# Seven block products in place of eight for gate and up of the last 1024 tokens of an encoder layer

## The chip, the cores and the metric

The kernel runs on one core of one Trainium2 chip, as one program of 36,635 instructions. The metric is the device time of one execution in microseconds (us); before the change the median of three runs is 2945.6 us (2943.91 to 2950.24).

## The reference, cut to what matters

One encoder layer over 2048 tokens with 1024 channels, all in float32: three mixers (a top-k latent attention, a gated linear attention and a sliding-window attention), an output projection, and then a feed-forward block with 2816 inner channels. The change touches the feed-forward block alone:

```python
x = x + jnp.concatenate([out_a, out_b, out_c], axis=-1) @ w_out
h = rms_norm(x, norm_ffn)
x = x + (jax.nn.silu(h @ w_ffn_gate) * (h @ w_ffn_up)) @ w_ffn_down
return rms_norm(x, final_norm)          # D_MODEL 1024, D_FF 2816, SEQ 2048
```

## The kernel before, in words

**Tiles.** Channels lie on the 128 partitions and tokens along the free axis. A group is 512 tokens; there are four groups. Every large product is done to nearly float32 precision by three matmuls: each operand is split into a part `hi`, rounded to the type that TensorE takes (float32r), and the rest `lo`, and hi·hi, lo·hi and hi·lo are summed in PSUM (L175 to L177 for the products over 8 blocks of input channels, L299 to L301 for the down projection). The split of a tile of 128x512 is one cast on ScalarE (L116) and one subtraction on GpSimd (L119). `square`, `norm_scale` and `finish` are the pieces of the RMS norm.

**Stages.** First come the projections and the mixers of all groups (`pass1`, `pass2`). The top-k attention (`dsa`: `select` and `attend` of 16 blocks of 128 queries) runs beside them and beside the feed-forward blocks of groups 0 and 1, which are done one group at a time, with tiles named `mf` in PSUM. The function `merge` interleaves these two threads by their estimated costs. When all 16 blocks are attended, the memory of the first part is given back, and the feed-forward block of groups 2 and 3 runs alone, with both groups in one pass (`halves` of 512 tokens, `W` = 1024, tiles named `pf`). This is the last stage.

**Inside `ffn`.** First `w_out` is applied and the residual added (L215 to L218), for half 0 and then for half 1; `normed` (L220) scales and splits the result into the operands `h2` of a half: a multiplication on VectorE (L229), a cast on ScalarE (L231), a subtraction on GpSimd or VectorE (L232), eight times. Then 22 steps `gate_up(f)`, each for 128 inner channels: 24 matmuls for gate and 24 for up, per half; tanh on ScalarE (L277), two combinations on VectorE (L278, L283) and the split of the result into `fh` and `fl`. `down` (L287) takes two steps at a time and adds to the residual `x2` on VectorE (L302).

**Weights.** The first feed-forward block (group 0) loads each weight tile, 128x512 float32, splits it and stores the halves, 512 KB, in DRAM; all later blocks load the stored halves (L131), into 5 buffers beside the attention and 9 in the last stage. All DMAs go through SyncE's queue. A weight tile of gate or up serves 12 matmuls per half.

**Order.** The program issues its instructions in the order of the generators, but each engine's queue is arranged when the kernel is built, by what is ready, with the program's order as priority; the queues are then run strictly in that arranged order.

## Time and profile before

| | us |
|---|---|
| median of 3 runs | 2945.6 |
| the profiled execution | 2950.48 |
| its span | 2948.7 |
| TensorE / VectorE / ScalarE / GpSimd busy | 2761.6 / 1677.2 / 1181.1 / 582.8 |
| first feed-forward block, gate and up (group 0) | about 1056 to 1501 |
| second (group 1) | about 1608 to 2049 |
| last stage (groups 2 and 3) | about 2103.5 to 2948.7 |

Times in the rows are microseconds from the start of the span. PE is TensorE, PEld its weight load, DVE VectorE, ACT ScalarE, POOL GpSimd, SPq SyncE's queue of DMA issues. In a table of stages each engine has its busy time and, in brackets, its instructions; then the granted clock of TensorE (1.00 is 2.4 GHz), the busy share of the DMA engines and what they moved. A busy matmul row overlaps the next one, so its mean is longer than the step from one to the next. The brackets at the end of a timeline row give the idle time before it and what ended it.

### The profile page before, as it was taken

To read this page: it belongs to the slowest core of one execution; us is meant where nothing else is said; L and a number is where in the kernel's file an instruction comes from. 1 tells how busy PE (TensorE), PEld (TensorE's weight loads), DVE (VectorE), ACT (ScalarE), POOL (GpSimd) and SP (SyncE) were. 2 spreads that over 40 slices of the span, in tenths; PEclk is the share of its full clock that TensorE was granted. 3 is DMA by queue.
4 is the path that set the end of the run, shared out by engine and by line. 5 is a ranking of instruction groups with operands and counts; after the bars stand their busy time and mean duration, and the time that the engine had idled before them with its cause. 6 is when DMAs were issued, how large, how long until landed. Compare 5 with 4: busy or idle time off the path is not lost.

```text
span 2948.7 us, 36635 instructions
## 1 busy us (share of the span) xinstructions
PE 2761.6 (94%) x13372; PEld 2171.4 (74%) x13372; DVE 1677.2 (57%) x3567; ACT 1181.1 (40%) x2061; POOL 582.8 (20%) x497
## 2 busy tenths in 40 slices
PE   7898999999999899999989999999899999999997
PEld 5666767676776767777767777777677888888886
DVE  3787887788767867475576673673342222222226
ACT  4655664665546655354553431441341000000004
POOL 3113420010100544444431100001111000000002
PEclk9998999999999989999999999999999999999998
DMA  7665534243332756666655444444572323323222
GB/s 248 193 190 191 183 122 142 92 149 106 103 128 78 268 179 229 227 214 225 226 187 193 142 150 143 137 152 147 188 249 87 108 92 100 100 86 107 93 93 72
DMA packets 179300, 451.12 MB, mean 153 GB/s; under 512 B 18632, under 2 KB 50288, under 8 KB 179120
## 3 DMA queue, kind: packets, MB, share of 16 engines
q1 hardware_dynamic: 179120, 448.78, 46.1%
q8 instruction: 105, 1.72, 0.2%
q14 instruction: 75, 0.61, 0.1%
HBM read 325.88 MB, written 122.83 MB: 152 GB/s over the span
## 4 chain that ended last, share of the span: by engine, by line
PE 59%; DVE 19%; ACT 8%; issue 7%; DMA 4%; POOL 2%; SPq 0%; DVEq 0%; ACTq 0%; POOLq 0%
PE pf L175 6%; PE pf L177 6%; PE pf L176 6%; DVE jd L937 6%; ACT jd L935 4%; PE mf L177 4%; PE mf L175 4%; PE mf L176 4%; PE pf L301 2%; PE pf L300 2%; PE pf L299 2%; PE mm L507 2%; PE mm L506 2%; PE mm L508 2%; PE mf L299 2%
## 5 line engine op out<-in xcount | busy, mean ns | idle before, releaser
L935 ACT ACTIVATE jd<-x,c 128x384 bf16<-128x384 f32 (+13 forms) x224 | 292.8, 1307 | 288.5 <-DVE c L962 228.7
L177 PE MATMUL mf<-al,w 128*128 128x512 f32 x832 | 329.1, 396 | 8.3 <-DVE al L212 4.1
L175 PE MATMUL mf<-ah,w 128*128 128x512 f32 x832 | 331.5, 399 | 3.7 <-ACT ah L231 2.8
L937 DVE TENSOR_SCALAR_CACHE_REDUCE jd<-x,c 128x384 bf16<-128x384 f32 (+13 forms) x224 | 330.9, 1477 | 6.5 <-DVE c L946 0.5
L175 PE MATMUL pf<-ah,w 128*128 128x512 f32 x832 | 325.1, 391 | 6.2 <-DMA w<-w 4.5
L119 POOL TENSOR_TENSOR w<-raw,w 128x512 fp32r<-128x512 f32 x192 | 260.0, 1362 | 341.4 <-ACT w L116 297.0
L176 PE MATMUL mf<-ah,w 128*128 128x512 f32 x832 | 327.4, 395 | 0.0
L177 PE MATMUL pf<-al,w 128*128 128x512 f32 x832 | 324.8, 391 | 1.3 <-POOL al L212 0.6
L176 PE MATMUL pf<-ah,w 128*128 128x512 f32 x832 | 325.3, 391 | 0.0
L119 POOL TENSOR_TENSOR fl<-u,fh 128x512 fp32r<-128x512 f32 x88 | 114.2, 1298 | 948.5 <-ACT fh L116 948.4
L506 PE MATMUL mm<-hh,w 128*128 128x512 f32 x576 | 241.3, 419 | 4.3 <-issue 2.0
L507 PE MATMUL mm<-hh,w 128*128 128x512 f32 x576 | 232.2, 403 | 0.6 <-POOL w L119 0.6
L508 PE MATMUL mm<-hl,w 128*128 128x512 f32 x576 | 230.9, 401 | 0.0
L177 PEld LDWEIGHTS mf<-al,w 128*128 128x128 f32 x832 | 158.5, 191 | 46.4 <-DVE al L212 4.5
L175 PEld LDWEIGHTS mf<-ah,w 128*128 128x128 f32 x832 | 159.0, 191 | 38.4 <-ACT ah L231 3.4
L175 PEld LDWEIGHTS pf<-ah,w 128*128 128x128 f32 x832 | 156.9, 189 | 39.9 <-DMA w<-w 4.9
L302 DVE TENSOR_TENSOR x<-x,pf 128x512 f32<-128x512 f32 (+1 forms) x184 | 121.9, 663 | 110.3 <-PE pf L301 110.0
L177 PEld LDWEIGHTS pf<-al,w 128*128 128x128 f32 x832 | 156.8, 188 | 35.9 <-POOL al L212 1.0
L176 PEld LDWEIGHTS mf<-ah,w 128*128 128x128 f32 x832 | 158.5, 190 | 31.7
L176 PEld LDWEIGHTS pf<-ah,w 128*128 128x128 f32 x832 | 156.8, 188 | 32.8 <-issue 0.5
L116 ACT CAST fh<-u 128x512 fp32r<-128x512 f32 x88 | 54.6, 620 | 308.1 <-DVE u L283 307.6
L299 PE MATMUL mf<-fh,w 128*128 128x512 f32 x352 | 147.0, 418 | 32.7 <-DVE x L302 17.3
(256 smaller groups left out, 5473.1 us busy)
## 6 DMA issues: line engine op xcount, KB each, us to landing
w<-w SPq DMA_DIRECT2D x636, 512.0 KB, 3.5
xk<-in_xT_dram SPq DMA_DIRECT2D x64, 256.0 KB, 3.3
raw<-in_w_in_dram SPq DMA_DIRECT2D x44, 256.0 KB, 3.7
raw<-in_w_g_dram SPq DMA_DIRECT2D x44, 256.0 KB, 3.7
raw<-in_w_u_dram SPq DMA_DIRECT2D x44, 256.0 KB, 3.9
raw<-in_w_d_dram SPq DMA_DIRECT2D x44, 256.0 KB, 4.3
m<-mixT SPq DMA_DIRECT2D x32, 256.0 KB, 3.1
x<-in_xT_dram SPq DMA_DIRECT2D x32, 256.0 KB, 4.6
```

Of the source, the lines that this page charges most:

```text
L119: Q.tensor_sub(lo, src, hi.bitcast(F32))
L175: T.matmul(ps, a, act[k][0], start=(first and k == ks[0]), stop=False)
L176: T.matmul(ps, b, act[k][0], start=False, stop=False)
L177: T.matmul(ps, a, act[k][1], start=False, stop=(last and k == ks[-1]))
L299: T.matmul(ps, hi[:, os_], ah[:, hs], start=(j == 0), stop=False)
L300: T.matmul(ps, lo[:, os_], ah[:, hs], start=False, stop=False)
L302: V.tensor_add(x2[:, oc, hs], x2[:, oc, hs], ps)
L506: T.matmul(ps, a, hh, start=(k == 0), stop=False)
L507: T.matmul(ps, b, hh, start=False, stop=False)
L508: T.matmul(ps, a, hl, start=False, stop=(k == KC - 1))
L935: A.activation(jd, xs, AF.Sign, scale=-1.0, bias=c[:, 0:1], accum_out=cnt)
L937: V.tensor_scalar(out=jd, in0=xs, scalar1=c[:, 0:1], scalar2=0.0, op0=ALU.is_ge, op1=ALU.add, accum_out=cnt)
```

## The change

In the last stage gate and up are no longer computed per 128 inner channels and half, but in 2x2 blocks: two steps f and f+1 (rows `r` of weights), two halves of the 1024 input channels, and the two halves of the tokens. The eight block products of such a square become seven (`seventh`, 12 matmuls each): four use sums of weight blocks (`s1` to `s4`) and sums of operand blocks (`t1` to `t4`), the others the blocks themselves. `quad` does one square and adds the products up on VectorE; `take_gate` and `take_up` do what followed a product before.

The sums of weights are made beforehand, while group 1's gate and up run: `summed_halves` loads four weight blocks (256 KB each), does four additions or subtractions on GpSimd, splits each sum and stores its halves (512 KB), in all 88 loads, 88 sums and 88 stores. It is advanced by three steps after each product of `gate_up`, five steps making up one set of four sums. The sums of operands are made once, in `first_halves` and `second_halves`, and the first square of gate and of up is done by `first_quads`. In the last stage the order is now gate of f and f+1, `down` of the pair before, up of f and f+1. Weight buffers there go from 9 to 6, the buffers of `fh`/`fl` from 4 to 2, those of the scratch tiles `m` from 3 to 8; in the first feed-forward blocks the raw weight buffers go from 3 to 4.

```diff
+    def summed_halves(srcs, raw_pool, n_raw, pool):
+        late = []
+        def leave(key, x):
+            if len(late) > 1:
+                nc.sync.dma_start(out=late[0][0], in_=late[0][1].bitcast(F32))
+                late.pop(0)
+            w = pool.tile([P, 1024], F32R, tag="ws", bufs=2, name="ws")
+            split(x, w[:, 0:512], w[:, 512:1024])
+            halved[key] = dram.tile([P, 1024], F32, name=f"w{len(halved)}")
+            late.append((halved[key], w))
+        for f in range(0, NF, 2):
+            for src in srcs:
+                a = {}
+                for r in range(2):
+                    for i in range(2):
+                        a[r, i] = raw_pool.tile([P, 512], F32, tag="raw", bufs=n_raw, name="raw")
+                        nc.sync.dma_start(out=a[r, i], in_=src[f + r][:, i * 512:(i + 1) * 512])
+                yield
+                s1, s2, s3, s4 = a[1, 1], a[0, 0], a[1, 0], a[0, 1]
+                for n, out, x, y, op in ((1, s1, a[1, 0], a[1, 1], ALU.add), (3, s3, a[0, 0], a[1, 0], ALU.subtract),
+                                         (2, s2, s1, a[0, 0], ALU.subtract), (4, s4, a[0, 1], s2, ALU.subtract)):
+                    Q.tensor_tensor(out=out, in0=x, in1=y, op=op)
+                    leave((src.tensor.name, f, f"s{n}"), out)
+                    yield
...
+        def both(j, x, eng):
+            hi, lo = pair(j)
+            A.copy(hi, x)
+            eng.tensor_sub(lo, x, hi.bitcast(F32))
+            return hi, lo
...
+        def second_halves():
+            norm_scale(halves[1])
+            for k in range(4):
+                b12, b22, t1, t2, t3, t4 = (temp() for _ in range(6))
+                scaled(k, 1, b12)
+                scaled(k + 4, 1, b22)
+                V.tensor_sub(t1, b12, kept[k])
+                hb["t1"].append(both(16 + k, t1, Q))
+                V.tensor_sub(t2, b22, t1)
+                hb["t2"].append(both(24 + k, t2, V))
+                V.tensor_sub(t3, b22, b12)
+                hb["t3"].append(both(8 + k, t3, Q))
+                V.tensor_sub(t4, kept[k + 4], t2)
+                hb["t4"].append(both(20 + k, t4, Q))
+                hb["b22"].append(both(12 + k, b22, V))
+                yield
...
+        def quad(src, f, take):
+            p1 = temp()
+            A.copy(p1, seventh(weight(src, f, "a11"), "b11"))
+            yield 2.7
+            u2 = temp()
+            V.tensor_add(u2, p1, seventh(weight(src, f, "s2"), "t2"))
+            yield 2.7
+            u3 = temp()
+            V.tensor_add(u3, u2, seventh(weight(src, f, "s3"), "t3"))
+            yield 2.7
+            p5 = seventh(weight(src, f, "s1"), "t1")
+            c22 = temp()
+            V.tensor_add(c22, u3, p5)
+            V.tensor_add(u2, u2, p5)
+            take(f, 1, 1, c22)
+            yield 2.7
+            V.tensor_add(p1, p1, seventh(weight(src, f, "a12"), "b21"))
+            take(f, 0, 0, p1)
+            yield 2.7
+            yield from ends_of(src, f, take, u2, u3)    # s4 by b22, a22 by t4
...
+        def first_quads():
...
+            ws = [[(b, weight(src, 0, a)) for b, a in (("t1", "s1"), ("t2", "s2"), ("t3", "s3"))] for src, _ in sides]
+            ps = [[ps_f() for _ in w] for w in ws]
+            for k in range(4):
+                for pp_, w_ in zip(ps, ws):
+                    for p_, (b, w) in zip(pp_, w_):
+                        part(p_, w, hb[b][k], k, k == 0, k == 3)
+                next(coming, None)
...
-            yield from gate_up(f)
-            if f and n_act < 4:
+            if nh == 1:
+                yield from gate_up(f)
+                if f:
+                    yield from down([f - 2, f - 1], steps)
+                yield from gate_up(f + 1)
+            elif f == 0:
+                yield from first_quads()
+            else:
+                yield from quad(w_g, f, take_gate)
                 yield from down([f - 2, f - 1], steps)
-            yield from gate_up(f + 1)
-            if f and n_act >= 4:
-                yield from down([f - 2, f - 1], steps)
+                room(f)
+                yield from quad(w_u, f, take_up)
```

## Rows read from the trace of the kernel before

**Rows 1.** The page: busy time by engine, and the chain that ended last.
```profile
PE 2761.6 (94%) x13372; PEld 2171.4 (74%) x13372; DVE 1677.2 (57%) x3567; ACT 1181.1 (40%) x2061; POOL 582.8 (20%) x497
...
PE 59%; DVE 19%; ACT 8%; issue 7%; DMA 4%; POOL 2%; SPq 0%; DVEq 0%; ACTq 0%; POOLq 0%
```

**Rows 2.** Busy time by stage: group 0, group 1, then four stretches of the last.
```profile
1056.00:1500.90 444.90, 423.38 (x2065) 341.41 (x2065) 271.38 (x533) 228.43 (x349) 203.32 (x161) 0.98 0.65 223
1608.20:2049.40 441.20, 418.00 (x2040) 337.74 (x2039) 252.39 (x459) 146.59 (x192) 33.89 (x32) 0.98 0.46 150
2103.50:2201.50 98.00, 91.69 (x387) 74.11 (x388) 35.48 (x47) 26.21 (x40) 14.84 (x11) 0.97 0.82 284
2201.50:2240.00 38.50, 37.13 (x159) 29.14 (x158) 15.84 (x20) 12.93 (x19) 9.84 (x7) 1.00 0.24 80
2240.00:2880.00 640.00, 640.00 (x2826) 530.10 (x2825) 155.11 (x226) 49.38 (x81) 51.99 (x41) 1.00 0.30 98
```

**Rows 3.** The page's costliest groups: one of three lines of 832 matmuls.
```profile
L175 PE MATMUL pf<-ah,w 128*128 128x512 f32 x832 | 325.1, 391 | 6.2 <-DMA w<-w 4.5
```

**Rows 4.** Groups by line, 2201.5 to 2932: busy us, mean ns, idle before.
```profile
L302 DVE TENSOR_TENSOR x<-x,pf 128x512 f32<-128x512 f32 (+1 forms) x183 | 121.5, 665 | 110.3 <-PE pf L301 110.0
...
L119 POOL TENSOR_TENSOR fl<-u,fh 128x512 fp32r<-128x512 f32 x44 | 57.0, 1296 | 605.3 <-ACT fh L116 605.3
L283 DVE SCALAR_TENSOR_TENSOR u<-s,pf 128x512 f32<-128x512 f32 x44 | 30.3, 688 | 180.0 <-PE pf L177 180.0
...
L116 ACT CAST fh<-u 128x512 fp32r<-128x512 f32 x44 | 27.3, 622 | 242.6 <-DVE u L283 242.6
```

**Rows 5.** VectorE in time, half 1's last residual and its scaling: start, us.
```profile
2201.55 0.69 DVE L217 TENSOR_TENSOR x<-x,pf 128x512 f32<-128x512 f32 x1 [3.30 <-PE pf L177]
...
2207.57 2.08 DVE L229 SCALAR_TENSOR_TENSOR hf<-x,vc,rs 128x512 f32<-128x512 f32 x3 [3.89 <-ACT rs L149]
2210.84 1.76 DVE L229 SCALAR_TENSOR_TENSOR hf<-x,vc,rs 128x512 f32<-128x512 f32 x1 [1.19 <-POOL al L232]
...
2219.34 1.18 DVE L232 TENSOR_TENSOR al<-hf,ah 128x512 fp32r<-128x512 f32 x1
```

**Rows 6.** GpSimd in time, the same stretch.
```profile
2209.11 2.94 POOL L232 TENSOR_TENSOR al<-hf,ah 128x512 fp32r<-128x512 f32 x2 [33.49 <-ACT ah L231]
2214.79 1.55 POOL L232 TENSOR_TENSOR al<-hf,ah 128x512 fp32r<-128x512 f32 x1 [2.74 <-ACT ah L231]
```

**Rows 7.** What TensorE waited for in the last stage: us in total, times, longest.
```profile
PE pm L202 <- DVE rs L197: 12.4, 3, 6.5
PE pf L175 <- DMA w<-w: 4.5, 1, 4.5
```

**Rows 8.** TensorE in time, inside one product of group 1.
```profile
1837.05 0.40 PE L175 MATMUL mf<-ah,w 128*128 128x512 f32 x1
1837.29 0.42 PE L1030 MATMUL sc<-cTh,lh 128*128 128x512 f32 x1
1837.54 0.39 PE L176 MATMUL mf<-ah,w 128*128 128x512 f32 x1
```

**Rows 9.** SyncE's queue in time, where the last stage begins.
```profile
2102.61 0.87 SPq L210 DMA_DIRECT2D m<-mixT  x2
2103.58 0.38 SPq L1088 DMA_DIRECT2D mixT<-ma  x1
```

**Rows 10.** DMA issues of group 1's stage: KB each, us to landing.
```profile
w<-w SPq DMA_DIRECT2D x125, 512.0 KB, 3.5
```

**Rows 11.** DMA of 2103.5 to 2201.5: GB/s in 40 slices.
```profile
GB/s 273 241 410 420 418 408 159 191 105 355 309 364 399 196 271 296 389 245 288 246 288 242 328 365 403 408 409 336 217 328 199 304 219 214 216 145 264 100 268 114
```

**Rows 12.** Groups by line in group 1's stage, ScalarE and VectorE.
```profile
L935 ACT ACTIVATE jd<-x,c 128x1920 bf16<-128x1920 f32 (+1 forms) x32 | 62.3, 1948 | 81.1 <-DVE c L962 60.5 <-DVE c L946 13.1 <-DVE c L952 7.4
...
L906 DVE SCALAR_TENSOR_TENSOR x<-r,w_tok,x 128x512 f32<-128x512 f32 x18 | 14.1, 786 | 6.2 <-ACT r L905 5.4
```

**Rows 13.** SyncE's waits in group 0's stage, 1100 to 1560.
```profile
SPq L144 <- POOL w L119: 293.1, 112, 8.9
```

More of the change, by code (lines that the diff above doesn't have):

```diff
@@ L1 @@
 from contextlib import ExitStack
+from itertools import islice
 import numpy as np
@@ L144, in store_halves @@
         nc.sync.dma_start(out=dst, in_=w.bitcast(F32))
+    def summed_halves(srcs, raw_pool, n_raw, pool):
[22 more added lines that the diff above has]
+                    yield
+        for dst, w in late:
+            nc.sync.dma_start(out=dst, in_=w.bitcast(F32))
     def rstd_of(ss, n, dst):
@@ L182, in ffn, with pair @@
         sparse, others = range(2), range(2, KC)
+        def pair(j):
+            pool = (fs if j % 8 < 2 else fo if j < 8 else fb) if j < 16 else fb
+            return tuple(pool.tile([P, 512], F32R, tag=f"b{j}{c}", bufs=1, name=f"a{c}") for c in "hl")
         def operand(i, k):
+            if nh == 2:
+                return pair(8 * i + k)
             pool = fo if k in others else fs
@@ L233, in normed, with temp, scaled @@
                 yield 0.4
+        def temp():
+            return fr.tile([P, 512], F32, tag="m", bufs=n_m, name="t")
+        def scaled(k, i, dst):
+            V.scalar_tensor_tensor(out=dst, in0=x2[:, k, halves[i]], scalar=vc[:, V_FFN + k:V_FFN + k + 1],
+                                   in1=rs[:, halves[i]], op0=ALU.mult, op1=ALU.mult)
+        def both(j, x, eng):
[3 more added lines that the diff above has]
+            return hi, lo
@@ new lines, in ffn, with first_halves @@
+        hb = {n: [] for n in ("b11", "b21", "b22", "t1", "t2", "t3", "t4")}
+        kept = []
+        def first_halves():
+            norm_scale(halves[0])
+            for k in range(KC):
+                kept.append(fb.tile([P, 512], F32, tag=f"b{16 + k}l", bufs=1, name="hf"))
+                scaled(k, 0, kept[k])
+                hb["b11" if k < 4 else "b21"].append(both(k, kept[k], V if k % 2 else Q))
+                yield 0.4
+        def second_halves():
[14 more added lines that the diff above has]
+                yield
@@ new lines, in weight, with part @@
+        def weight(src, f, a):
+            r, i = {"a11": (0, 0), "a12": (0, 1), "a22": (1, 1)}.get(a, (0, a))
+            return load_halves((src.tensor.name, f + r, i), None, None, 0, fh, n_w)
+        def part(ps, w, b, k, first, last):
+            hi, lo = w
+            x, y = (t[:, k * P:(k + 1) * P] for t in (hi, lo))
+            T.matmul(ps, x, b[0], start=first, stop=False)
+            T.matmul(ps, y, b[0], start=False, stop=False)
+            T.matmul(ps, x, b[1], start=False, stop=last)
@@ new lines, in seventh, with take_gate, take_up @@
+        def seventh(w, b):
+            ps = ps_f()
+            for k in range(4):
+                part(ps, w, hb[b][k], k, k == 0, k == 3)
+            return ps
+        gated = {}
+        def take_gate(f, r, i, z):
+            t = temp()
+            A.activation(t, z, AF.Tanh, scale=0.5)
+            gated[r, i] = ft.tile([P, 512], F32, tag="g", bufs=4, name="g")
+            V.scalar_tensor_tensor(out=gated[r, i], in0=t, scalar=1.0, in1=z, op0=ALU.add, op1=ALU.mult)
+        def take_up(f, r, i, z):
+            u = temp()
+            V.scalar_tensor_tensor(out=u, in0=gated[r, i], scalar=0.5, in1=z, op0=ALU.mult, op1=ALU.mult)
+            ah, al = acts[f + r]
+            split(u, ah[:, halves[i]], al[:, halves[i]])
@@ new lines, in room @@
+        def room(f):
+            for f_ in (f, f + 1):
+                acts[f_] = tuple(ft.tile([P, W], F32R, tag=f"f{c}", bufs=2, name=f"f{c}") for c in "hl")
+        def quad(src, f, take):
[18 more added lines that the diff above has]
+            yield from ends_of(src, f, take, u2, u3)
@@ new lines, in ends_of @@
+        def ends_of(src, f, take, u4, u3):
+            V.tensor_add(u4, u4, seventh(weight(src, f, "s4"), "b22"))
+            take(f, 0, 1, u4)
+            yield 2.7
+            V.tensor_add(u3, u3, seventh(weight(src, f, "a22"), "t4"))
+            take(f, 1, 0, u3)
+            yield 2.7
+        def first_quads():
+            sides = ((w_g, take_gate), (w_u, take_up))
+            p1 = [ft.tile([P, 512], F32, tag="p1", bufs=2, name="p1") for _ in sides]
+            for x, (src, _) in zip(p1, sides):
+                A.copy(x, seventh(weight(src, 0, "a11"), "b11"))
+            room(0)
+            coming = second_halves()
+            next(coming)
+            for x, (src, take) in zip(p1, sides):
+                c11 = temp()
+                V.tensor_add(c11, x, seventh(weight(src, 0, "a12"), "b21"))
+                take(0, 0, 0, c11)
+            ws = [[(b, weight(src, 0, a)) for b, a in (("t1", "s1"), ("t2", "s2"), ("t3", "s3"))] for src, _ in sides]
+            ps = [[ps_f() for _ in w] for w in ws]
+            for k in range(4):
+                for pp_, w_ in zip(ps, ws):
+                    for p_, (b, w) in zip(pp_, w_):
+                        part(p_, w, hb[b][k], k, k == 0, k == 3)
+                next(coming, None)
+                yield 4.1
+            for (src, take), (p5, p6, p7), x in zip(sides, ps, p1):
+                u2, u3, c22 = temp(), temp(), temp()
+                V.tensor_add(u2, x, p6)
+                V.tensor_add(u3, u2, p7)
+                V.tensor_add(c22, u3, p5)
+                V.tensor_add(u2, u2, p5)
+                take(0, 1, 1, c22)
+                yield from ends_of(src, 0, take, u2, u3)
```

32 lines of the change are left out of this document (19 added, 13 removed).

## The prediction, made before the changed kernel was run

> **What bounds the kernel now.** I read the page first. TensorE is busy 94% of the span, and 59% of the chain that ended last is its work [rows 1]. But busy shares are means over stages, so I read the stages next. In the last stage, from 2240 to 2880, TensorE is busy for all of 640.00 us, at full granted clock, with 2826 matmuls [rows 2]: 0.2265 us from one to the next, and nothing waits. There a matmul taken away is time taken away. Beside it VectorE has 155 us of work in 640, ScalarE 49, GpSimd 52, and the DMA engines are busy for 0.30. The stage of group 1, where the sums of weights are to be made, is another matter: TensorE is busy 418.0 of 441.2 us, VectorE 252, ScalarE 147, GpSimd only 34, and 150 GB/s are moved [rows 2]. What TensorE waits for in the last stage is little: 4.5 us for a weight tile at its start and 12.4 us for norms, most of it in the tail [rows 7].
>
> **What goes: 264 matmuls.** The three lines of the products in tiles `pf` have 832 matmuls each [rows 3], 2496 in all. The output projection has 8 x 2 x 24 = 384 of these; gate and up have 2112 = 22 x 2 x 2 x 24. After the change they are 22 squares of 7 products of 12 matmuls, 1848. The 264 that go, by 0.2265 us, are **-59.8 us**, if TensorE stays as densely fed as now.
>
> **Is it still fed in the steady part?** A square takes TensorE 84 x 0.2265 = 19.0 us. VectorE gets seven additions that were not there, at 0.665 us (as L302), and four combinations at 0.69 (as L283), which it had before [rows 4]: 7.4 us of 19. In all 22 x 7 x 0.665 = 102 us more, against 485 us in which it is idle now between 2240 and 2880. ScalarE gets one copy per square, as long as a cast, 0.62 us. All this lies beside matmuls, and with 7 PSUM buffers a product needn't wait for the addition behind it. If that cover were gone, one exposed addition per product would cost 154 x 0.67 = 103 us; nothing in the stage points to it, since the 183 additions of L302 already run behind `down` with VectorE idle between them. The weights cost more: a pair of steps loads 14 tiles for gate and up in place of 8, and 4 for `down`, 18 x 0.524 MB in 168 + 96 matmuls, 59.8 us: 158 GB/s in place of 98. A tile now lasts 12 matmuls, 2.7 us, in place of 24, and 6 buffers are five tiles or 13.6 us ahead of TensorE; a tile lands 3.5 us after its issue [rows 10]. I take nothing for it; the other end stands among the rivals.
>
> **Where the stage begins: the sums of operands.** Before, the second half's operands are made from 2207.57 to 2220.52 [rows 5], and TensorE hardly sees it, since it has gate and up of half 0 to do. Their cost is peculiar. A VectorE operation that reads two tiles from SBUF takes 0.69 us alone (three in 2.08) but 1.76 us when a subtraction of GpSimd runs, which itself takes 1.3 us alone [rows 4 to 6]. The two exclude each other: eight multiplications and four subtractions on VectorE at some 0.65, 7.8 us, and four on GpSimd at 1.3, 5.2 us, add up to 13.0, and 12.95 were measured. `second_halves` has per k eight such operations on VectorE (two `scaled`, four differences, two `lo`) and three on GpSimd: 8 x 0.65 + 3 x 1.3 = 9.1 us, and four times that is 36.4 us, from 2207.6 to 2244. TensorE has until then: four products without `t` operands (10.9 us) and six with (16.3 us), which from the last residual at 2201.5 would end at 2228.7. It now ends some 1.5 us behind the last `t3`, about 2245.5, thus 17 us late. About 2 us of small waits that TensorE has there now (0.7 us for a cast, and shorter ones) go into this. **+15 us.** Bounds: if nothing excludes anything, VectorE's 21 us end at 2228.4 and the cost is 1 us; if casts between the operations aren't hidden, and TensorE's clock falls in its pauses, I put 24.
> The Trainium skill, SBUF — State Buffer, "Who interferes with whom", states the same as a lock: a VectorE instruction with two SBUF inputs and a GpSimd instruction that reads SBUF use one port pair, and whoever comes second blocks fully. The trace agrees (1.76 us for 0.69). By that rule the 36.4 us stand; by a reader's guess that five engines overlap they would be 21.
>
> **What comes early or late besides.** The last square is now followed directly by the last `down`, where before a whole `down` lay between. The last result needs an addition, a combination, a cast and a subtraction: 0.67 + 0.69 + 0.62 + 1.30 = 3.3 us [rows 4]; TensorE can meanwhile do the first step's share of four outputs, 12 matmuls or 2.7 us. **+1**, at most 3. The wait of 4.5 us for weights at the stage's start may go, since the buffers lie elsewhere; I count it only for the lower end.
>
> **What the preparation costs group 1.** Each of 88 sums is two operations of GpSimd, 1.3 us each, and a cast of 0.62 us on ScalarE; with three steps after each product, 110 steps are done after 18.3 of 22 steps f. GpSimd's load rises by 229 us, from 34 of 441 to some 60% busy; ScalarE's by 55 us; the DMAs by 88 x 0.262 + 88 x 0.524 = 69 MB. Of a step's 21 us (441.2/21) the new share is 3.8 MB, the old 3.1 MB: about 325 GB/s, where slices of 400 to 420 are seen [rows 11]. None of this waits for TensorE or makes it wait by itself. What can suffer is the chain of probes of `select`, on ScalarE and VectorE in turn: ScalarE idles 81.1 us before 32 probes, 2.5 us each [rows 12], so a cast fits in if it comes at the right time and delays a probe by up to 0.62 if not. Upper end: all 55 us on the chain, and each of the 27 or so VectorE operations with two SBUF inputs (21 of them L906, by its two shapes) behind a sum for 0.8 us, 76 us together. Lower end: nothing. The nearest row is the stage of group 0: with ScalarE busy 228 us, GpSimd 203 and 223 GB/s it loses 21.5 us of TensorE in 444.9, no more than group 1's 23.2 in 441.2 [rows 2]. I stay near it: about a seventh of the casts' time, **+8 us**. The fourth raw buffer in group 0's stage I take as nothing.
>
> Of queues: the stores of the sums and the loads of raw weights stand in SyncE's queue among the weight loads. In the order of the lines, a store that waits for GpSimd, which waits for a cast behind tanh, would hold up the next product's weights. The trace shows that queues are not in that order: inside the twelve matmuls of a product, which are issued together, a matmul of the attention stands at L1030 [rows 8], and two loads of the last stage went ahead of a store of the attention that was issued earlier but not ready [rows 9]. In group 0's stage SyncE waited 293 us for such stores [rows 13], and TensorE was fed.
>
> **Sum.** -59.8 + 15 + 1 + 8 = -35.8 us. Against the profiled execution, 2950.5 (span 2948.7), 2914.7; this execution was 4.9 us above the median, so of medians **2910**. All lower ends: 2945.6 - 59.8 + 1 - 4.5 = 2882; all upper ends: -59.8 + 24 + 3 + 76 = +43, 2989.
>
> **Rivals.**
> - *Full gain* (0.20): the sums of operands and of weights are hidden, for the planned order puts GpSimd's parts where VectorE reads PSUM. For it: VectorE also has additions out of PSUM in that stretch. Against: the 13.0 us that added up. -59.8 + 2: 2888.
> - *Weights late* (0.12): with five tiles ahead in place of eight, and twice the tiles, one wait per square. For it: a first tile was waited for 4.5 us [rows 7]. Against: 158 GB/s is far from the 420 seen [rows 11]. At 1.6 us for each of 22 squares, +35: 2945, no change.
> - *The preparation blocks* (0.18): the planned order is wrong by the real durations, and a weight load of group 1 stands behind a store whose sum isn't ready: GpSimd 1.3, cast 0.62, GpSimd 1.3, 3.2 us more than planned, in each of 18.3 steps, 59 us, with the 15 and 1 from above: -59.8 + 16 + 59 + 8 = +23, **2969, slower**. It decides from 44/18.3 = 2.4 us per step. For it: the queue's waits of up to 8.9 us [rows 13]; against: five weight buffers ahead, and group 0's stage.
> - That the sums come too late for the last stage is excluded: 18.3 steps are done before 22.
>
> **Chances.** Forecast 0.50, with 2893 to 2930 of its own. A measurement here can't tell less than 0.2%, 5.9 us. Faster: 0.50 + 0.20 + 0.05 of the third case = 0.75; within: 0.05 of the third and 0.05 of the last = 0.10; slower 0.15. Range 2884 to 2952: it leaves out the best end of full gain and most of the last case.
>
> **What would show it.** Right: 1848 matmuls of gate and up in the last stage at 0.2265 us; from the last residual to the end of the six `t` products about 44 us, with TensorE waiting for GpSimd or VectorE there; group 1's stage at 441 to 456 us with no wait of TensorE for weights. Wrong: TensorE waiting for DMA in the squares (weights late), or L175 waiting for a weight tile in group 1 (the preparation blocks), or VectorE's differences at 0.65 us beside a busy GpSimd (full gain).

## The result, and the profile after

The change makes the kernel slower: 2969.7 us (median of 4 runs, 2966.1 to 2973.2) against 2947.9 us (4 runs, 2943.9 to 2950.4), a ratio of 1.0076 with a 95% interval of 1.0062 to 1.0091. The prediction was 2910, with a range of 2884 to 2952. Below, "stage of group 1" is the stretch from group 1's first tanh to the first matmul of the last stage, and "its gate and up" the part of it from the first tanh to the last.

The page of the changed kernel, engines and the chain that ended last [rows 1]:

```profile
PE 2729.9 (92%) x13108; PEld 2130.5 (72%) x13108; DVE 1838.2 (62%) x3741; ACT 1247.1 (42%) x2183; POOL 834.1 (28%) x681
...
PE 42%; DVE 7%; DMA 6%; POOL 4%; issue 3%; ACT 3%; SPq 0%; ACTq 0%; POOLq 0%; DVEq 0%
```

The shares of this chain add up to 65%, for it could be followed back only to 1051 us; before they add up to 99%, so 42% isn't to be held against the 59%. From 1051 us on, where there is a chain in both, TensorE has 1240 us of it in place of 1317, DMAs 171 in place of 44 and GpSimd 113 in place of 46: DMAs and GpSimd came in. Where that happened is read from the stages [rows 2]; the first two rows are a stretch ahead of group 1's first tanh and group 1's gate and up, the others the last stage:

```profile
1501.00:1608.00 107.00, 86.13 (x396) 63.99 (x395) 80.82 (x123) 54.28 (x82) 43.09 (x31) 0.90 0.69 238
1624.00:2114.00 490.00, 433.99 (x2039) 343.64 (x2038) 265.99 (x459) 189.10 (x268) 238.66 (x185) 0.95 0.75 259
2200.00:2260.00 60.00, 59.00 (x259) 48.17 (x258) 32.46 (x41) 21.81 (x33) 12.57 (x8) 1.00 0.70 235
2260.00:2300.00 40.00, 30.00 (x98) 20.93 (x96) 31.75 (x33) 16.68 (x25) 16.98 (x10) 0.83 0.23 66
2300.00:2880.00 580.00, 578.47 (x2549) 478.36 (x2550) 265.77 (x379) 64.31 (x105) 55.37 (x42) 1.00 0.50 163
```

Before, the first of these stretches and the whole stage of group 1 were:

```profile
1501.00:1608.00 107.00, 92.50 (x432) 69.79 (x431) 82.53 (x133) 54.35 (x81) 22.42 (x16) 0.95 0.53 180
1608.20:2103.50 495.30, 468.05 (x2368) 375.92 (x2366) 283.15 (x521) 177.47 (x236) 43.29 (x40) 0.98 0.44 143
```

Group 1's first tanh comes at 1624.0 in place of 1608.2, and its gate and up take 490 us in place of 441. The last stage begins at 2168.2 in place of 2103.6 and takes 778.8 us to its last matmul in place of 827.7. So 65 us were lost ahead of the last stage and 49 won in it. The last stage itself did what was forecast:

```profile
L328 PE MATMUL pf<-ah,w 128*128 128x512 f32 x616 | 242.5, 394 | 5.3 <-ACT ah L285 5.3
L330 PE MATMUL pf<-al,w 128*128 128x512 f32 x616 | 242.3, 394 | 6.2 <-DVE al L286 3.7 <-POOL al L286 2.5
```

616 matmuls on each of three lines are the 1848 of the sum, and the row of 2300 to 2880 has one each 0.2275 us, with TensorE busy 578 of 580 us at 163 GB/s. The start of that stage, one step k of `second_halves` on VectorE [rows 5]:

```profile
2289.05 1.40 DVE L280 SCALAR_TENSOR_TENSOR t<-x,vc,rs 128x512 f32<-128x512 f32 x2
2290.38 0.68 DVE L309 TENSOR_TENSOR t<-t,hf 128x512 f32<-128x512 f32 x1
...
2292.30 1.78 DVE L315 TENSOR_TENSOR t<-hf,t 128x512 f32<-128x512 f32 x1
2294.00 3.46 DVE L286 TENSOR_TENSOR al<-t,ah 128x512 fp32r<-128x512 f32 x2
2297.39 1.41 DVE L280 SCALAR_TENSOR_TENSOR t<-x,vc,rs 128x512 f32<-128x512 f32 x2
```

From one k to the next it is 8.34 us (2289.05 to 2297.39), where 9.1 were forecast. The last three operations take 5.2 us while three subtractions run on GpSimd (5.13 us from 2291.78 on), and 2.1 would be three at 0.69.

What TensorE, SyncE's queue and ScalarE waited for between 1501 and the start of the last stage (total us, times, longest):

```profile
PE tr L1240 <- ACT big L1231: 17.2, 5, 8.5
PE mf L486 <- DMA w<-w: 15.6, 8, 3.9
PE mf L208 <- DMA w<-w: 13.0, 6, 5.0
```
```profile
SPq L154 <- POOL ws L120: 163.0, 40, 10.7
SPq L132 <- PE mf L210: 93.5, 43, 7.3
...
SPq L167 <- POOL ws L120: 66.1, 29, 6.4
```
```profile
ACT ws L117 <- DMA w<-ws: 86.2, 34, 16.6
```

Before, SyncE waited there for TensorE to give weight buffers back: it was ahead.

```profile
SPq L131 <- PE mf L177: 266.5, 88, 11.4
```

Without the preparation it does so still ("SPq L133 <- PE mf L211: 255.6, 86, 11.1" in the last version below). Now it stands 229 us at stores whose sums aren't split yet (L154) and at raw loads whose buffers these splits still read (L167), and TensorE waits 28.6 us for weights, 0 before. GpSimd in time, where group 0's gate and up have just ended and then up to the first tanh:

```profile
1506.53 1.28 POOL L120 TENSOR_TENSOR fl<-u,fh 128x512 fp32r<-128x512 f32 x1 [4.08 <-ACT fh L117]
1509.73 5.73 POOL L172 TENSOR_TENSOR raw<-raw 128x512 f32<-128x512 f32 x4 [1.91 <-issue]
1515.42 2.55 POOL L120 TENSOR_TENSOR ws<-raw,ws 128x512 fp32r<-128x512 f32 x2
...
1539.58 6.39 POOL L172 TENSOR_TENSOR raw<-raw 128x512 f32<-128x512 f32 x4
1545.93 1.26 POOL L252 TENSOR_TENSOR al<-m,ah 128x512 fp32r<-128x512 f32 x1
...
1618.64 1.67 POOL L272 TENSOR_TENSOR al<-hf,ah 128x512 fp32r<-128x512 f32 x1 [1.28 <-ACT ah L271]
```

Sums of weights (L172) run 114 us ahead of the first tanh behind which the program issues them, and among them stand the operands that group 1 needs to begin. The third `al` of the mixer outputs (L252) comes behind four sums, at 1545.93 where it was 1538.51 before; the last `al` of the normed operands (L272), behind sums and splits, ends at 1620.3. Before it ended at 1606.3:

```profile
1604.60 1.67 POOL L232 TENSOR_TENSOR al<-hf,ah 128x512 fp32r<-128x512 f32 x1 [1.52 <-ACT ah L231]
```

### The profile page after: what moved, and what is told of

The parts are those of the page before. It is cut to its first block, busy times and chain, and to the rows that moved or that the text cites. A ratio compares the mean times of both kernels' runs of the same rounds, so it can differ in the third digit from the quotient of the medians.

```text
span 2964.2 us, 37368 instructions
## 1 busy us (share of the span) xinstructions
PE 2729.9 (92%) x13108; PEld 2130.5 (72%) x13108; DVE 1838.2 (62%) x3741; ACT 1247.1 (42%) x2183; POOL 834.1 (28%) x681
## 4 chain that ended last, share of the span: by engine, by line
PE 42%; DVE 7%; DMA 6%; POOL 4%; issue 3%; ACT 3%; SPq 0%; ACTq 0%; POOLq 0%; DVEq 0%
PE pf L330 5%; PE pf L328 5%; PE pf L329 5%; PE mf L210 3%; PE mf L208 3%; PE mf L209 3%; PE pf L488 3%; PE pf L487 3%; PE pf L486 3%; DMA w<-ws 2%; DVE jd L1130 2%; PE mf L486 2%; POOL raw L172 2%; PE mf L488 2%; PE mf L487 1%
## 5 line engine op out<-in xcount | busy, mean ns | idle before, releaser
L208 PE MATMUL mf<-ah,w 128*128 128x512 f32 x832 | 335.7, 404 | 19.6 <-DMA w<-w 13.0
L209 PE MATMUL mf<-ah,w 128*128 128x512 f32 x832 | 331.0, 399 | 0.0
L330 PE MATMUL pf<-al,w 128*128 128x512 f32 x616 | 242.3, 394 | 6.2 <-DVE al L286 3.7
L328 PE MATMUL pf<-ah,w 128*128 128x512 f32 x616 | 242.5, 394 | 5.3 <-ACT ah L285 5.3
L329 PE MATMUL pf<-ah,w 128*128 128x512 f32 x616 | 241.7, 393 | 0.0
L120 POOL TENSOR_TENSOR fl<-t,fh 128x512 fp32r<-128x512 f32 x44 | 57.1, 1299 | 562.7 <-ACT fh L117 549.4
L117 ACT CAST w<-raw 128x512 fp32r<-128x512 f32 x192 | 115.7, 615 | 108.0 <-PE mf L210 40.8
L120 POOL TENSOR_TENSOR ws<-raw,ws 128x512 fp32r<-128x512 f32 x88 | 120.7, 1379 | 127.2 <-ACT ws L117 127.2
L489 DVE TENSOR_TENSOR x<-x,mf 128x512 f32<-128x512 f32 x176 | 118.3, 682 | 52.9 <-PE mf L488 52.7
L172 POOL TENSOR_TENSOR raw<-raw 128x512 f32<-128x512 f32 x88 | 119.3, 1356 | 97.5 <-DMA raw<-in_w_g_dram 52.9
```

The costliest lines, as they stand in the source:

```text
L120: Q.tensor_sub(lo, src, hi.bitcast(F32))
L208: T.matmul(ps, a, act[k][0], start=(first and k == ks[0]), stop=False)
L209: T.matmul(ps, b, act[k][0], start=False, stop=False)
L328: T.matmul(ps, x, b[0], start=first, stop=False)
L329: T.matmul(ps, y, b[0], start=False, stop=False)
L330: T.matmul(ps, x, b[1], start=False, stop=last)
```

## The experiments

Three causes stand against each other for the 65 us. *Order*: GpSimd's queue, arranged ahead of time, has sums in front of what group 1 needs. *Waits for results*: a cast, store or load of the preparation stands at the head of its engine's queue until another engine's result is there, and what is behind it stands too. *Load*: transfers and engines are simply busier. The stage of group 1 holds the same matmuls, 2367 to 2369 in the records, in every kernel of which its row is shown below, so its length, TensorE's busy time, the granted clock and the DMA rate compare directly.

**Nothing prepared.** The sums' keys point at plain halves, and all else is as in the change, the fourth raw buffer too.

```diff
-   (summed_halves: loads, sums, splits, stores)
+   halved[src.tensor.name, f, f"s{n}"] = halved[src.tensor.name, f + (n - 1) // 2, (n - 1) % 2]
```


> The change without its preparation: no sums of weights are loaded, added, split or stored in group 1's stage; where the last stage needs the halves of a sum it loads the stored halves of a plain block, so the numbers are not the layer's. All theories agree that the last stage, from its first matmul to its last, stays near the 778.8 us of the changed kernel (827.7 before). Theory A (the preparation costs what was lost): the way to the last stage's first matmul falls back from 2168 to about 2104 us, and the whole to 2947.9 - 49 = about 2899 us. Theory B (the fourth raw buffer or the other memory layout of the first part costs): the first matmul stays above 2125 us, and the whole above 2920 us.

Measured: 2900.6 us, ratio 0.9839 (0.9824 to 0.9854). The stage of group 1 is as before the change, 495 us:

```profile
1610.10:2105.20 495.10, 467.01 (x2367) 375.62 (x2365) 285.85 (x524) 179.67 (x241) 46.79 (x42) 0.98 0.46 151
```

So the preparation costs 69 us, and without it the change is worth 48; the prediction's other terms, -59.8 + 15 + 1 = -43.8, were near. The buffers, which are as in the change, cost nothing to be seen.

**One ingredient at a time.** Only the 88 loads and 88 stores, of a tile that is always ready; only the casts; sums and splits without DMAs; only GpSimd's 176 operations.

```diff
-   Q.tensor_tensor(...); split(x, w[:, 0:512], w[:, 512:1024])
+   # DMAs alone:   neither; w = zeros, loaded tiles unused
+   # casts alone:  A.copy(w[:, 0:512], out)
+   # sums + splits: always the same four raw tiles, no stores
+   # GpSimd alone: Q.tensor_tensor(...); Q.tensor_sub(w[:, 512:1024], out, x)
```


> The preparation's 88 loads of 256 KB and 88 stores of 512 KB alone, with no sum and no split: the stores send a tile of zeros that is always ready, so nothing on SyncE's queue waits for GpSimd, and ScalarE and GpSimd have nothing to do for it; the last stage then works with zeros as sums. If DMA bandwidth is the cost (a weight tile of group 1 took 5.7 us to land in the changed kernel, 3.5 before): TensorE still waits for weights in group 1, the first matmul of the last stage stays within 15 us of 2168, the whole at 2955 us or more. If it is the waits in the queues (SyncE waited 229 us for GpSimd, ScalarE's casts 86 us for the stores that free their buffers): the first matmul at 2104 to 2120 us, the whole at 2900 to 2915 us.

> Of the preparation only the 88 casts, on ScalarE as in the change, from raw tiles that are loaded once and always ready: no sums, no subtractions, no stores; the last stage loads plain blocks' halves, so the numbers are not the layer's. Theory W (what costs is that a cast in ScalarE's queue waits for GpSimd or for a store, with the attention's and the feed-forward's ScalarE work behind it): casts that never wait cost little, the whole at 2900 to 2915 us. Theory T (the casts' own time on a full chain, 55 us): 2940 to 2956 us.

> The other half: the 88 sums and 88 splits, in place on four raw tiles that are loaded once, and none of the preparation's other loads and none of its stores; the last stage loads plain blocks' halves in place of the sums, so the numbers are not the layer's. If GpSimd's and ScalarE's time, and the exclusion of VectorE operations with two SBUF inputs, is the cost: the first matmul of the last stage stays at 2150 us or more and the whole at 2945 or more. If it is DMA bandwidth or waits that hang on the DMAs: first matmul at 2104 to 2125 us, the whole 2900 to 2920 us. If it divides, this run and the one with DMAs alone add up to about 65 us over the run without preparation.

> Of the preparation only the 176 additions and subtractions on GpSimd, in place on raw tiles loaded once: no casts, no other loads, no stores; the last stage loads plain blocks' halves. Theory W: nothing of ScalarE waits for GpSimd's sums now; GpSimd is as busy as before, and VectorE operations with two SBUF inputs still stand behind it: 2903 to 2925 us. Theory P (GpSimd's load and the exclusion of VectorE is the cost): 2960 us or more, near the 3036 us of the run with casts, additions and subtractions.

Measured: 2904.9 us (ratio 0.9847, 0.9830 to 0.9863), 2905.0 (0.9846, 0.9832 to 0.9861), 3036.1 (1.0294, 1.0279 to 1.0310) and 3034.2 (1.0284, 1.0267 to 1.0302). The two halves, DMAs alone (4 us over nothing prepared) and sums with splits (135), don't add up to the 69. GpSimd's operations alone cost more than the whole change. In their run TensorE waits, ahead of group 1's gate and up, for GpSimd's own subtractions (`al` of the mixer outputs and of the normed operands), and one stretch shows the state of all:

```profile
PE mf L197 <- POOL al L259: 70.9, 3, 64.5
PE mf L197 <- POOL al L239: 45.0, 3, 26.4
```
```profile
1608.00:1738.00 130.00, 49.83 (x197) 35.76 (x196) 53.21 (x48) 17.88 (x27) 126.56 (x94) 0.65 0.17 56
1738.00:2181.00 443.00, 418.57 (x2040) 338.59 (x2040) 255.19 (x459) 146.74 (x191) 64.17 (x56) 0.97 0.46 149
```

GpSimd is busy 126.6 of 130 us, TensorE 49.8; once the sums are over, gate and up take 443 us as before. A caution on the first two: nothing holds such work back, so it ran early. Of the 88 stores only 19 lie between 1608 and 2050 (203 GB/s there), and 73 of the 88 casts lie ahead of 1611. The whole stage of group 1 with DMAs alone:

```profile
1610.20:2105.30 495.10, 468.30 (x2369) 376.76 (x2367) 285.79 (x524) 180.01 (x241) 46.76 (x42) 0.97 0.59 196
```

These two runs don't show the cost of that work *beside* group 1's products; a later run does.

**Three variants of the whole change:** its DMAs issued from GpSimd's queue; the sums cast on GpSimd; four buffers for the sums' halves in place of two.

```diff
-   nc.sync.dma_start(...)                            # in summed_halves
+   Q.dma_start(...)                                  # first variant
-   split(x, w[:, 0:512], w[:, 512:1024])
+   split(x, w[:, 0:512], w[:, 512:1024], Q)          # second
-   w = pool.tile([P, 1024], F32R, tag="ws", bufs=2, name="ws")
+   w = pool.tile([P, 1024], F32R, tag="ws", bufs=4, name="ws")   # third
```


> The whole change, with the preparation's loads and stores issued from GpSimd's queue in place of SyncE's: no weight load of group 1 stands behind a store that waits for a sum. If the blocking of SyncE's queue is the main cost: TensorE's waits for weights in group 1 (28.6 us in 14 waits) go, the first matmul of the last stage comes by 2125 us, the whole at 2920 us or less. If it is ScalarE's casts that wait for the stores (86 us) or bandwidth: little changes, 2955 to 2980 us; issuing from GpSimd may cost its own time there, which would show as more busy time or gaps of GpSimd.

> The whole change, with the casts of the sums on GpSimd too in place of ScalarE: one edit, 88 casts moved. GpSimd then has about 3.8 us per sum, 340 us in all, and its sums wait for loads and stores as before, but no other engine waits for GpSimd in its own queue except SyncE. Theory W: the way to the last stage's first matmul falls from 2168 to 2105 to 2125 us, and the whole to 2901 to 2922 us, faster than both kernels. If SyncE's blocked queue is the cost: TensorE's waits for weights stay (28.6 us), the whole at 2935 to 2975 us. If GpSimd's load is: above 2965 us.

> The whole change with four buffers for the prepared halves in place of two, nothing else. It takes away the 86 us in which casts wait for a store to free their buffer, and leaves those in which they wait for GpSimd's sum (34 us). Theory W with the stores as its larger part: the whole falls by 25 to 50 us, 2920 to 2945 us. If the casts then only wait for GpSimd instead, because the plan packs them closer (as in the run without loads and stores): 2960 to 3040 us, no better or worse.

Measured: 3070.8 (ratio 1.0416, 1.0400 to 1.0431), 2976.9 (1.0089, 1.0074 to 1.0104) and 2963.7 us (1.0047, 1.0032 to 1.0062). Issued from GpSimd's queue the DMAs leave the weights free, and TensorE waits 0.3 us for them in place of 28.6; yet this is 101 us worse than the change. Each issue takes 0.55 us of GpSimd's own time, 96 us in all, and ScalarE's casts stand 270 us for sums and stores in place of 120. Neither forecast held, and weights behind stores can't be the main cost. With the casts on GpSimd no cast stands on ScalarE, but SyncE still stands 244 us at stores and raw loads and TensorE waits 38 us for weights: the forecast of 2901 to 2922 failed. With four buffers ScalarE's casts no longer wait for stores (6.5 us in place of 86.2) but for sums (103.6 in place of 34.3), and about 6 us are won: a wait taken away comes back as the next one.

**GpSimd's operations in the program's order.** Each sum and its `lo` is queued behind the `fl` subtraction that group 1 issued last; first for GpSimd's operations alone, then for the whole change, with two and four buffers.

```diff
-   for _ in islice(prepare, 3): pass
+   with tc.issue_after(mark[-1]):     # the last split's subtraction: an edge for the order, no wait
+       for _ in islice(prepare, 3): pass
```


> As the run with the 176 GpSimd operations alone (no casts, loads or stores; the last stage takes plain halves as s1 to s4, so its values differ), but each operation is queued on GpSimd behind the subtraction of `fl` that group 1's gate and up issued last, an edge for the order alone. Theory of the order (GpSimd's queue was planned with the sums ahead of what group 1 needs to begin): the first tanh of group 1 comes back from 1738.8 to about 1610, the first matmul of the last stage from 2235.3 to 2105 to 2130, the time to 2903 to 2930 us. Rival, the load (176 x 1.3 to 1.4 us on GpSimd, and VectorE shut out meanwhile, cost the same wherever they lie): the first tanh is back at 1610, but gate and up take 560 instead of 441 us, first matmul of the last stage at 2220 to 2240, 3020 to 3035 us.

> The whole change, each sum and its `lo` queued on GpSimd behind the last `fl` subtraction issued by group 1's gate and up. Theory of the order: of the 65 us that the preparation cost, the 18 ahead of the first tanh go (1624.0 to about 1608), and a part of the 49 behind it; first matmul of the last stage at 2120 to 2150, time 2925 to 2955 us. Rival, ScalarE's casts that wait for a store to land (86 us, up to 16.6 at a time) and weights behind stores in SyncE's queue make up the 49: they are untouched, first tanh at 1608 but first matmul of the last stage at 2150 to 2168, 2950 to 2970 us. Rival, the load: no change, 2965 to 2972.

> As the one before, with four buffers for the sums' halves in place of two. If the casts' waits for stores are what is left of the 49 us, this comes 15 us or more below the one before (with the order alone left as it was, four buffers gave 6 us); by the theory of the order at most 5 below it, 2920 to 2950 us.

Measured: 2921.1 us (one time) for GpSimd alone, in place of 3034.2: of 133 us, 113 were order. Its stage of group 1:

```profile
1611.30:2122.10 510.80, 472.79 (x2368) 378.80 (x2366) 301.96 (x524) 180.09 (x241) 284.29 (x218) 0.96 0.44 146
```

But the whole change gets worse: 3005.5 us (1.0181, 1.0156 to 1.0205) and 3006.5 (1.0189, 1.0168 to 1.0211). Group 1 does begin early again (first tanh at 1608.7 in place of 1624.0), and then its stage takes 602 us, with the clock down to 0.91:

```profile
1608.70:2211.00 602.30, 504.17 (x2368) 395.44 (x2366) 299.70 (x524) 228.79 (x329) 280.66 (x218) 0.91 0.69 237
```
```profile
ACT ws L117 <- POOL raw L172: 103.0, 38, 8.2
ACT ws L117 <- DMA w<-ws: 72.4, 23, 14.7
```

All forecasts for the whole change failed. An edge on one engine seems to have moved the standing to another: only GpSimd's instructions were held back, and ScalarE, which `select`'s probes need too, stands 175 us at casts of the sums in place of 120. TensorE's waits for weights rose as well, from 28.6 to 46.4 us. The next runs take the two apart.

**Which coupling?** Sums and splits in that order without DMAs; then the whole change in that order with casts on GpSimd and four buffers; then, as the first, but each sum in one of four buffers of its own and cast one product later, behind ScalarE's last instruction for group 1.

```diff
+   for x in made:                     # sums of the product before
+       A.copy(w[:, 0:512], x); Q.tensor_sub(w[:, 512:1024], x, w[:, 0:512].bitcast(F32))
+   for ... in sums[:2]: Q.tensor_tensor(out=made[-1], ...)
```


> Sums and splits without loads and stores (always the same four blocks, so the last stage's values differ), with GpSimd's operations queued behind the last `fl` subtraction that group 1's gate and up issued. If ScalarE, standing at casts for GpSimd's sums, makes the rest of the loss, it is there without any DMA: first matmul of the last stage at 2170 to 2215, 2970 to 3010 us. If the rest comes from buffers that wait for stores and loads, it is gone: first matmul of the last stage at 2120 to 2140, 2918 to 2935 us.

> The whole change, GpSimd's operations queued behind `fl` as before, the casts of sums on GpSimd too (0.75 us each in place of 0.62 on ScalarE), four buffers for sums. If ScalarE's standing at casts is what hurts (for a sum or for a store), this gives most of it back: first matmul of the last stage at 2120 to 2150, 2920 to 2950 us. If it is GpSimd's load and its queue (three operations per sum, 3.4 us, with the loads and stores waited for in it), then `fl` is as late as before: 2165 to 2215, 2965 to 3010 us.

> As the run of sums and splits in order and without loads and stores, but each sum is cast one product (some 10 us) after it was made, the cast queued on ScalarE behind group 1's last tanh or cast; two sums per product, the same 88 sums (the last two aren't split, and the last stage's values differ as there). If ScalarE's standing at casts makes the 49 us between GpSimd's operations alone (2921) and sums with splits (2970), most of it goes: first matmul of the last stage at 2118 to 2132, 2917 to 2931 us, and ScalarE waits for sums less than 20 us in all. If it is the load of the engines, nothing changes: 2160 to 2175, 2960 to 2975 us.

Measured: 2970.3 (one time), 3011.2 (1.0200, 1.0182 to 1.0217) and 2919.4 us (one time). Stages of the first and the last:

```profile
1604.50:2171.80 567.30, 482.24 (x2368) 384.06 (x2367) 301.63 (x524) 229.61 (x329) 280.20 (x218) 0.93 0.40 132
```
```profile
1609.20:2119.60 510.40, 472.54 (x2367) 378.23 (x2365) 301.67 (x524) 224.37 (x327) 279.87 (x214) 0.96 0.45 146
```

The work is nearly the same (GpSimd busy 280.2 and 279.9 us, ScalarE 229.6 and 224.4); 57 us of stage go with the waits. ScalarE's waits at these casts, of the first run and of the last:

```profile
ACT ws L117 <- POOL raw L159: 87.6, 53, 4.5
ACT ws L117 <- POOL ws L120: 53.0, 26, 5.9
```
```profile
ACT ws L161 <- POOL rawo L166: 16.1, 6, 8.0
ACT ws L161 <- POOL ws L162: 12.4, 5, 6.6
```

141 us in place of 28. With the casts on GpSimd the standing moved on to SyncE and to the weights; TensorE's waits in that run:

```profile
PE mf L492 <- DMA w<-w: 59.9, 15, 12.7
PE mf L208 <- DMA w<-w: 20.4, 5, 8.0
```

So queues that stand for results can be a real cost. What is left when that is gone, 15 us of stage, is no more than GpSimd's operations alone cost in that order (510.8 us), so the casts themselves add nothing to be seen.

**The load of the DMAs, in place.** The DMAs alone, each behind group 1's last weight load, so that they lie in group 1's stage; then these (with stores of a tile that is always ready) beside sums that are cast one product later: all the load, and hardly anything to wait for.

```diff
+   with tc.issue_after(mark["SP"]):   # the last weight load
+       (raw loads of 256 KB, stores of a ready tile)
```


> As the run of the 88 loads and 88 stores alone (nothing is summed, the stores hold zeros), but each is queued on SyncE behind the weight load that group 1 issued last, so that all lie in group 1's stage. If the weights are late because SyncE stands at stores that aren't ready, nothing is lost here: first matmul of the last stage at 2103 to 2112, 2900 to 2912 us, TensorE waiting for weights under 5 us. If it is the DMAs' load, TensorE waits for weights 20 to 50 us: 2920 to 2955 us.

> All the load of the preparation in group 1's stage with no instruction that must wait for another's result: sums cast one product later as in the run before (2919), and beside them two raw loads of 256 KB and two stores (each of 2 x 256 KB of a tile that is always ready) per product, queued behind the last weight load. Values of the last stage differ as there. If the loss of the change is instructions that stand in a queue for a result, this costs what the engines cost, 18 us, and a few: first matmul of the last stage at 2120 to 2135, 2919 to 2935 us. If the load as a whole makes it, 2960 to 3005 us.

Measured: 2942.8 and 2947.7 us (one time each, without an interval; 42 and 47 above the run with nothing prepared). Stages of the two, and of the change:

```profile
1610.50:2143.70 533.20, 486.44 (x2368) 384.04 (x2366) 287.97 (x524) 178.54 (x241) 47.43 (x42) 0.96 0.71 264
```
```profile
1608.70:2149.10 540.40, 486.71 (x2368) 384.88 (x2367) 302.44 (x524) 222.73 (x327) 274.18 (x214) 0.95 0.72 260
```
```profile
1624.00:2168.20 544.20, 484.11 (x2368) 381.81 (x2366) 299.43 (x524) 222.19 (x318) 251.54 (x195) 0.95 0.72 249
```

This was a miss for the theory of waits: DMAs that wait for nobody cost 38 us when they lie beside group 1's products at 264 GB/s, and all the load 45 (its time lies between its two forecasts). But TensorE waits for weights only 4 and 12 us in these runs, where 20 to 50 were forecast for the first. Half of the 38 us is idle time, in front of the attention's matmuls: 34 us of waits there between 1611 and 2091 in the run with DMAs alone, 8 with nothing prepared. The other half is the same matmuls, which are busy 19 us longer. Weight tiles land 7.0 us after issue (median) at a mean of 274 GB/s (1610 to 2090), 3.5 at 148:

```profile
PE o L1247 <- ACT pT L1239: 12.2, 6, 3.5
```
```profile
w<-w SPq DMA_DIRECT2D x124, 512.0 KB, 7.0
```

Whether the slow landings act on TensorE, or the order arranged with these transfers in it does (the attention of the last block but one ends 32 us earlier than with nothing prepared, the last tanh comes 40 later), isn't settled.

**The sums made in the last stage instead.** Only those of the first pair of steps are prepared in group 1's stage; otherwise the last stage loads the raw blocks and makes the sums one square ahead, on VectorE. The second version finds buffers for the start of the stage.

```diff
+   def sums(src, f):                  # four raw loads, then per sum, one square ahead:
+       V.tensor_tensor(out=out, in0=x, in1=y, op=op)
+       A.copy(hi, out); V.tensor_sub(lo, out, hi.bitcast(F32))
-   n_w = 6, m: 8 buffers
+   n_w = 4, m: 6, ws: 2, raw: 4      # second: w_out, b12, b22, t4 use ws and raw at first
```


> Nothing but the sums for the first pair of steps is prepared in group 1's stage; for the other ten pairs the last stage loads the four raw blocks (4 x 256 KB in place of 4 x 512 KB of halves) and makes the sums itself, sum and `lo` on VectorE (0.69 us each) and the cast on ScalarE, one square ahead, in two buffers. Four weight buffers in place of six, six scratch tiles in place of eight, and the products of a square in another order to suit. 80 x 2 x 0.69 = 110 us more on VectorE, which was busy 257 of 580 us there, and 50 on ScalarE (60 of 580). If the loss lies in group 1's stage alone, group 1 is as without preparation but for a tenth of it: first matmul of the last stage at 2105 to 2113, and with TensorE fed as densely as in the change 2902 to 2915 us. Rival: sums, casts and `lo` in turn come late, or VectorE's additions hold PSUM too long, some 1 us for each of 140 products: 3040 us; by four weight buffers alone, 1.5 us in each of 21 squares, 2935 us.

> As the version with the sums in the last stage, with buffers found for its start: two of each half's weight tiles for `w_out` in three go to the two buffers of the sums (idle until then), and the scaled operands `b12`, `b22` and the difference `t4` of `second_halves` to buffers of sums and of raw weights, so that two steps k fit at once, as in the change with eight scratch tiles. If the 13 us more in the last stage (793 against 780 us without any sums) were for want of buffers at its start, 8 to 13 of them go: 2908 to 2915 us. If they come from the sums' own work beside the squares, no change: 2920 to 2925 us.

Measured: 2922.9 us (ratio 0.9908, 0.9893 to 0.9923), above the forecast, then **2912.8 us** (0.9883, 0.9866 to 0.9899), within it: faster than both kernels. Of the second, the stage of group 1 and the body of the last:

```profile
1607.70:2101.30 493.60, 467.62 (x2368) 375.71 (x2367) 283.06 (x521) 177.98 (x238) 43.39 (x40) 0.98 0.46 150
```
```profile
2320.00:2880.00 560.00, 556.61 (x2490) 461.83 (x2489) 350.21 (x513) 118.22 (x198) 63.34 (x41) 1.00 0.36 117
```

In the last stage VectorE's busy share rises from 46% in the change (266 of 580) to 63% (350 of 560), and TensorE is still busy 556.6 of 560 us; the DMAs move 117 GB/s, less than in the change, for a raw block is half the size of its halves. Raw blocks cost 256 KB once, where the change moved 256 KB in, 512 out and 512 in again. The first version's last stage, first to last matmul, took 793 us against 780 with nothing prepared, the second 786. That VectorE is the place for such a sum is also what the Trainium skill, GPSIMD Engine Reference, "Engine selection", says (a two-input elementwise operation is about twice as slow on GpSimd); these traces agree, with 0.69 us against 1.30 alone.

## Why the prediction was wrong

- **Right: the matmuls.** -59.8 us for 264 matmuls at 0.2265 us: the last stage became 48.9 us shorter, where -59.8 + 15 + 1 gives -43.8. Most of the 5 us between them is the wait for a first weight tile at its start, 4.5 us before and 0.3 now, which the sum left out.
- **Right: the two engines excluding each other** in `second_halves`: 8.3 us per k, where 9.1 were worked out. TensorE waits 11.5 us for operands there in the rows, of the 15.
- **Right: weights in the squares.** TensorE waits for no weight tile between 2300 and 2880, at 163 GB/s; the tail cost 0.6 us.
- **The step that failed: +8 us for the preparation in group 1's stage.** It measured 65 in the profiled execution and 69 between the timed kernels, near the upper end that was worked out, 76, but for other reasons. Three things were wrong in it.
  First, the load. All of it with hardly anything to wait for costs 45 us of stage. The prediction compared the 325 GB/s needed with slices of 400 to 420 [rows 11] and took the room between for free. At 196 GB/s over the stage nothing was lost (the run of DMAs alone, when most had run early); at 264, 38 us. A rate reached in a few slices didn't tell what the stage bears as a mean. Group 0's stage, taken as the nearest row, ran at 223 GB/s [rows 2], between the two.
  Second, the place. GpSimd's load, "from 34 of 441 to some 60% busy", was reckoned in group 1's stage, but the arranged order put the first sums 114 us ahead of it, in front of `al`. The first tanh was 16 us late, and with GpSimd's operations held back it came at 1608.7.
  Third, "none of this waits for TensorE or makes it wait by itself" counted durations and not the chain raw load, sum, cast, `lo`, store over four in-order queues. Rows 8 and 9 do show that the queues are not in the program's order, and the sum took that as cover, with nothing for an instruction that stands. But an instruction is overtaken only in the arrangement, made beforehand; in the run what is queued behind it stands too, as ScalarE did for 120 us at casts of the sums. In the change itself this seems to add little to the other two (544 us of stage, 540 with hardly a wait); with GpSimd's order alone mended the stage is longest (602).
- **The rival "the preparation blocks"** gave 2969, the time measured, by 3.2 us per step at a store in SyncE's queue. The standing store is there (229 us of SyncE's waits), but it made TensorE wait for weights 28.6 us and not 59, stores that are always ready cost most of the same, and with the stores in another queue these waits were gone and the kernel slower still. That its price came out right is luck.
- What stays open: 16 us ahead of the stage, 45 of load and about 4 more are in step with the 65 us, but the parts were measured in other arrangements, two of them in a single execution, and they don't add up in general (15 and 38 alone, 45 together). How the transfers lengthen the stage is open too, and no run of the whole change holds GpSimd's sums and ScalarE's casts back together.

## What to carry to other kernels

Price work that is moved into an idle engine's time by the whole chain that it brings, each step at the queue where it stands, and by the transfers at the stage's mean rate against one at which this stage was seen to be fed, not by the engine's idle share. Before building such a preparation ask whether the stage that uses the result has a free engine: there it needs no store and no reload. An edge for the order on one engine alone can make things worse; without DMAs in the way it helped to move the consumer on the next engine back with it.

## What was unexpected in the hardware

- A weight tile of 512 KB lands 3.5 us after its issue at a mean of 148 GB/s and 3.6 at 203, but 5.6 at 259 (in the change) and 7.0 at 274: twice the time for a third more rate.
- Waiting costs twice. The 2368 matmuls of group 1's stage were busy for 467 us where TensorE stood 28 us (clock 0.98) and for 504 where it stood 98 (clock 0.91): of 107 us lost, 37 are the same matmuls taking longer.
- VectorE and GpSimd shut each other out in a mixed stage too: 176 more operations on GpSimd raised VectorE's busy time in the stage from 286 to 302 us. That is 16 us, or 0.09 for each; the prediction's upper end had 27 operations by 0.8, 22 us.
